# The head of a hybrid trunk kernel: squares summed on VectorE, one norm chain, GpSimd's elementwise work moved, and a step-size chain moved one weight pair later

## The chip, the cores and the metric

The kernel runs on one core of one Trainium2 chip. The metric is the device time of one execution in microseconds (us); a kernel is given by the median of its runs. Engines are named as in the profile: PE (TensorE matmuls), PEld (its weight loads), DVE (VectorE), ACT (ScalarE), POOL (GpSimd), SP (SyncE, which here only issues DMAs).

## The reference

One layer of a hybrid sequence model, on x of 1024 frames by 1024 channels, in float32, and a final RMSNorm. Cut to the part that the change touches:

```python
c_act = silu(c)
mod = (c_act @ w_ada + b_ada).reshape(1, 6, 1024)   # shift1, scale1, gate1, shift2, scale2, gate2
u = rms_norm(x, ln1) * (1.0 + scale1) + shift1
proj = u @ w_in                                      # 11296 columns: gates, conv, z, xBC, dt
...
dt = softplus(dt + dt_bias)
a = -exp(a_log)                                      # the state-space scan uses xs * dt and dt * a
```

Behind it come two mixers, two branch projections, the merge by gates, an output projection and an MLP of width 4096.

## The kernel before

Everything is held transposed: 128 channels on the partitions, 1024 frames along the free dimension, in two halves h of 512. x is eight channel tiles k of two halves each, 16 tiles `xt[k][h]`. A float32 matmul of full precision is made of three float32r matmuls: each operand is split into a high and a low part (`uh`, `ul` for u; `whi`, `wlo` for the weights), and high times high, high times low and low times high are added in PSUM (`mm3`, L108). The high part is a cast on ACT, the low part a subtraction on DVE.

The head, in the order of the code:

- L255 to L266: constants, and silu(c) broadcast to all partitions in `cb`.
- L276 to L279: SP issues the 16 loads of x and the two loads of the first modulation tile pair (`load_ada(0)`; each is 128 by 1024, 512 KB).
- L293 to L304: the norm, by half. `Stats.add` (L212) squares each of the eight tiles on ACT; for half 0 DVE adds the eight squares up in one tile, for half 1 POOL adds six of them and PE takes the last two as they are. `cols` (L205) sums over the partitions with matmuls of one column, 4 for each tile that it is given. Then a chain of some 11 small DVE operations (`rsqrt_eps`, L184: a seed and three Newton steps) gives 1/rms, DVE spreads it on a diagonal (`sdg`), a matmul with ones broadcasts it to all partitions, and ACT copies it to `rb`. So there are two such chains, one for each half. Behind that of half 0 stand three dummy matmuls (`WARM`).
- L312 to L332: the loop over the eight channel tiles j. Its modulation pair is loaded (four buffers, two for each j). `gemv` (L283) multiplies a 128 by 1024 tile of w_ada by `cb` and sums along the row, which gives shift or scale of 128 channels: for scale it is one DVE instruction, for shift from j = 1 on it is a POOL multiplication, an ACT pass that sums, and a small DVE operation. Then, for each half, DVE forms x times scale times `rb`, ACT adds the shift and casts it to `uh`, and DVE makes `ul`. In the first two rounds the weights of the first four feature tiles are split, with the low part on POOL. PE multiplies tile j of u by the four feature tiles (24 matmuls of 512 columns a round, 192 in all), into eight PSUM banks.
- L345 to L360: feature tiles 4 and 5 with `proj` (96 matmuls), while DVE and ACT make the operands of Strassen's scheme out of x (`tops_of` at L127, four DVE operations and four splits for each of four k; tiles named x and t).
- L362 to L383: the 32 dt columns: weights `wdr`, split to `wd`, 32 matmuls into `st`, then eight small matmuls (L383, 16 records) that turn the result and add its two parts.
- L392 to L412: softplus on a 128 by 256 tile as one DVE chain of about 25 operations, with two ACT passes near its start. It reads the PSUM tile `st` itself.
- L426 to L447: thirteen `strassen_pair`s (L135), for gates f = 6 to 15 and z. Each is seven products of 12 matmuls, with DVE sums of weight blocks (`s12`, `s34`), four weight splits and the evacuations. Between them stand three gemvs for each pair (`gemvs(3)`), out of 32 for the other four modulation vectors; they are loaded by POOL's DMA queue into one buffer `wv`.

Each engine takes its instructions strictly in the order of a list that is made when the kernel is built, by a planner that simulates the engines and takes, among the ready instructions of an engine, the one that stands first in the code. `tc.issue_after(i)` only adds an order: the instructions of the block on i's engine come behind i in its list.

Of the kernel before, what the change touches and what calls it, by code (L numbers as in the profile page):

```python
# [13 lines left out]
P = 128  # L14
T = 1024
# [7 lines left out]
WARM = 3  # L23
# [13 lines left out]
def hybrid_trunk(tc, xT, par, hrows, crow, wada1, wada2, win, wdt, wco, wso, wo, wup, wdn, out):  # L37
# [64 lines left out]
    def shift_split(hi, lo, src, col):  # L102
        act.activation(hi, src, AF.Identity, bias=col)
        stt(lo, src, col, hi.bitcast(F32), ALU.add, ALU.subtract)
# [166 lines left out]
    def load_ada(j):  # L271
        for q in (1, 0):
            wa[j, q] = p0.tile([P, T], F32, name="wada", bufs=4)
            sp.dma_start(wa[j, q], wada1[j, :, q])
# [4 lines left out]
    load_ada(0)  # L279
# [3 lines left out]
    def gemv(w_, o, eng):  # L283
        if eng is dve:
            dve.tensor_tensor_reduce(out=w_, in0=w_, in1=cb, scale=0.5, scalar=prm[:, BADA + o:BADA + o + 1],  # L285
                                     op0=ALU.mult, op1=ALU.add, accum_out=mcol[:, o:o + 1])
        else:
            tt(w_, w_, cb, ALU.mult, eng=pool)
            ga = p0.tile([P, 1], F32, name="ga")
            act.activation(w_, w_, AF.Copy, accum_out=ga)  # L290
            stt(mcol[:, o:o + 1], ga, 0.5, prm[:, BADA + o:BADA + o + 1], ALU.mult, ALU.add)

    rbs, sts = [], []  # L293
    for h in (0, 1):
        st = Stats(p0, ps0, pool if h else dve, 6 if h else 8, h)
        for k in range(KT):
            st.add(xt[k][h])
        rb = p0x.tile([P, H], F32, name=f"rb{h}")
        act.copy(rb, st.rb)
        rbs.append(rb)  # L300
        sts.append(st)
        if h == 0:
            for _ in range(WARM):
                pe.matmul(wps, lhsT=ones, rhs=xt[0][0], start=True, stop=True)  # L304
# [7 lines left out]
    for j in range(KT):  # L312
        if j:
            load_ada(j)
        if j in (0, 1):
            for f in range(2):
                ws.append(load_w(win[2 * j + f], eng=pool))
        with tc.issue_after((sts[0].dg if j else sts[0].last_add).ins):
            gemv(wa[j, 1], 8 + j, dve)
        gemv(wa[j, 0], j, pool if j else dve)  # L320
        stt(s1c[:, j:j + 1], mcol[:, 8 + j:9 + j], 1.0, prm[:, LN1 + j:LN1 + j + 1], ALU.add, ALU.mult)
        for h in (0, 1):
            x_ = xt[j][h]
            stt(x_, x_, s1c[:, j:j + 1], sts[0].rb if h == j == 0 else rbs[h], ALU.mult, ALU.mult)
            shift_split(uh[j][h], ul[j][h], x_, mcol[:, j:j + 1])
# [23 lines left out]
    for k in range(4):  # L349
        tks.append(tc.alloc_tile_pool(name=f"tk{k}", bufs=1, side="right", reuse_waits="tile"))  # L350
        for i, t in zip((0, 1, 2, 3), tops_of(xt[k] + xt[k + 4], mcol[:, 4 + k:5 + k], dc1[:, k:k + 1])):
# [42 lines left out]
    ev = sm("ev")
    act.activation(ev, v, AF.Abs)
    act.activation(ev, ev, AF.Exp, scale=-1.0)
    den = sm("den")
    tsc(den, ev, 2.0, None, ALU.add, ALU.bypass)
    dve.reciprocal(den, den)
    tt(ev, ev, den, ALU.mult)  # L400
    tt(z2, ev, ev, ALU.mult)
    tsc(den, z2, 2.0 / 19.0, 2.0 / 17.0, ALU.mult, ALU.add)
    for n in (15, 13, 11, 9, 7, 5, 3, 1):
        tt(den, den, z2, ALU.mult)
        tsc(den, den, 2.0 / n, None, ALU.add, ALU.bypass)
    tt(den, den, ev, ALU.mult)
    dtf = dt_t.rearrange("p c h -> p (c h)")
    stt(dtf, v, 0.0, den, ALU.max, ALU.add)
# [549 lines left out]
```

## Time and profile before

| | us |
|---|---|
| median of 3 runs (lowest, highest) | 2187.24 (2185.82, 2188.59) |
| the profiled execution's own time | 2188.47 |
| its span in the profile | 2186.7 |
| PE busy in the span | 2123.2 |
| DVE busy | 1409.7 |
| ACT busy | 876.8 |
| POOL busy | 146.1 |

The span runs from the first to the last instruction; 1.8 us of the execution's own time lie around it. Times of a row of the timeline are counted from the span's start. A row's second number is how long the instruction took, and the brackets, where there are any, say how long its engine had been idle and which event ended that. Windows of the trace give, for each engine, busy us and the number of instructions, then the clock that TensorE was granted (1.00 is full), the DMA engines' busy share and GB/s.

### The profile page before, as it was taken

The page shows a single profiled execution, that of the slowest core. Times are in us where ns is not written, and L with a number is a line of the kernel's source. Part 1 is how long each engine was busy: PE and PEld are TensorE (multiplying, and loading weights), DVE is VectorE, ACT ScalarE, POOL GpSimd, SP SyncE. Part 2 cuts the span into 40 slices and gives each one's busy share as a digit, 9 for nine tenths or more (in the row PEclk, how much of TensorE's full clock was granted, in tenths as well). Part 3 has the DMA queues.
Part 4 walks back from the last instruction along what each step waited for, and adds up shares of the span by engine and source line. Part 5 has one row for each costly group of instructions (what it writes and reads, how often), then busy time and mean ns, then how long its engine had stood idle before and what let it go on. Part 6 is the DMA issues. An engine that isn't in the chain of part 4 may idle for free.

```text
span 2186.7 us, 26107 instructions
## 1 busy us (share of the span) xinstructions
PE 2123.2 (97%) x9930; PEld 1734.7 (79%) x9930; DVE 1409.7 (64%) x2137; ACT 876.8 (40%) x1449; POOL 146.1 (7%) x216
## 2 busy tenths in 40 slices
PE   5989999999999999999999999999999999999998
PEld 3768778888888887888877888888788888888887
DVE  8947777664787767676785648746655545544444
ACT  4523333323565546364663421334445453211112
POOL 5100000000000000000000000021000000000003
PEclk7989999999999999999999999999999999999999
DMA  6325554223132322232347586543333336332212
GB/s 243 119 77 200 192 176 149 83 77 128 51 100 84 103 98 82 95 114 78 102 124 285 195 287 202 187 140 106 125 107 115 112 110 230 111 101 87 87 39 78
DMA packets 115471, 283.27 MB, mean 130 GB/s; under 512 B 10465, under 2 KB 45665, under 8 KB 115346
## 3 DMA queue, kind: packets, MB, share of 16 engines
q1 hardware_dynamic: 86882, 187.02, 26.7%
q0 software_dynamic: 16192, 58.73, 8.0%
q10 hardware_dynamic: 12272, 35.85, 4.2%
q8 instruction: 78, 1.28, 0.2%
q14 instruction: 47, 0.39, 0.1%
HBM read 218.45 MB, written 63.11 MB: 129 GB/s over the span
## 4 chain that ended last, share of the span: by engine, by line
PE 81%; issue 11%; DVE 5%; DMA 1%; POOL 1%; ACT 1%; SPq 0%; POOLq 0%; DVEq 0%; ACTq 0%
PE mm L144 21%; PE mm L113 18%; PE mm L111 18%; PE mm L110 18%; PE B L577 2%; PE B L582 1%; DVE x L45 1%; PE C L599 1%; PE A L554 1%; DMA wv<-in_wada 1%; DVE wada L285 1%; POOL wv L423 1%; DVE ul L45 1%; PE st L209 0%; DMA x<-in_xT 0%
## 5 line engine op out<-in xcount | busy, mean ns | idle before, releaser
L111 PE MATMUL mm<-ul,whi 128*128 128x512 f32 x768 | 304.9, 397 | 6.8 <-DVE ul L45 6.8
L144 PE MATMUL mm<-t,whi 128*128 128x512 f32 x944 | 294.4, 394 | 15.9 <-ACT whi L149 11.5
L110 PE MATMUL mm<-uh,whi 128*128 128x512 f32 x768 | 303.3, 397 | 2.5 <-ACT whi L93 2.5
L93 ACT CAST whi<-wraw 128x1024 fp32r<-128x1024 f32 x126 | 132.3, 1051 | 426.0 <-PE mm L111 402.1
L113 PE MATMUL mm<-uh,wlo 128*128 128x512 f32 x768 | 246.2, 396 | 0.1
L42 DVE TENSOR_TENSOR wlo<-wraw,whi 128x1024 fp32r<-128x1024 f32 (+1 forms) x188 | 212.0, 1128 | 41.2 <-ACT whi L93 35.1
L144 PEld LDWEIGHTS mm<-t,whi 128*128 128x128 f32 x944 | 179.0, 190 | 56.2 <-ACT whi L149 12.7
L45 DVE SCALAR_TENSOR_TENSOR y<-mm,mcol,y 128x512 f32<-128x512 f32 (+1 forms) x136 | 92.5, 716 | 157.6 <-PE mm L113 157.5
L144 PE MATMUL mm<-t,wlo 128*128 128x512 f32 x472 | 183.8, 391 | 0.0
L111 PEld LDWEIGHTS mm<-ul,whi 128*128 128x128 f32 x768 | 145.1, 189 | 36.9 <-DVE ul L45 7.7
L110 PEld LDWEIGHTS mm<-uh,whi 128*128 128x128 f32 x768 | 144.7, 189 | 33.9 <-ACT whi L93 3.3
L113 PEld LDWEIGHTS mm<-uh,wlo 128*128 128x128 f32 x768 | 144.7, 189 | 30.4 <-DVE wlo L42 0.5
L111 PE MATMUL mm<-hid,whi 128*128 128x512 f32 (+1 forms) x416 | 154.9, 374 | 0.0
L110 PE MATMUL mm<-hid,whi 128*128 128x512 f32 (+1 forms) x416 | 153.9, 373 | 0.0
L111 PE MATMUL mm<-ys,whi 128*128 128x512 f32 x384 | 148.5, 394 | 0.0
L110 PE MATMUL mm<-ys,whi 128*128 128x512 f32 x384 | 147.5, 395 | 0.6 <-ACT ys L99 0.5
L45 DVE SCALAR_TENSOR_TENSOR cacc<-raw,hw,cacc 128x1024 f32<-128x1024 f32 x96 | 122.8, 1279 | 27.9 <-ACT cacc L529 26.0
L144 PE MATMUL mm<-s,whi 128*128 128x512 f32 x448 | 137.8, 389 | 0.7 <-ACT cu L167 0.7
L113 PE MATMUL mm<-hid,wlo 128*128 128x512 f32 (+1 forms) x416 | 130.0, 373 | 0.0
L571 ACT ACTIVATE seg<-acb,acum 128x128 f32<-128x128 f32 x256 | 81.9, 392 | 102.6 <-PE B L577 95.0
L113 PE MATMUL mm<-ys,wlo 128*128 128x512 f32 x384 | 121.2, 390 | 0.0
L42 DVE TENSOR_TENSOR wlo<-s,whi 128x1024 fp32r<-128x1024 f32 x66 | 80.5, 1221 | 56.5 <-ACT whi L149 56.5
(269 smaller groups left out, 4027.8 us busy)
## 6 DMA issues: line engine op xcount, KB each, us to landing
wraw<-in_win SPq DMA_DIRECT2D x88, 512.0 KB, 3.5
wv<-in_wada POOLq DMA_DIRECT2D x32, 512.0 KB, 3.8
acb<-ac_d SPq DMA_DIRECT2D x64, 256.0 KB, 4.8
wraw<-in_wup SPq DMA_DIRECT2D x32, 512.0 KB, 3.6
hr<-hid_d POOLq DMA_DIRECT2D x32, 512.0 KB, 4.5
wraw<-in_wdn SPq DMA_DIRECT2D x32, 512.0 KB, 3.6
hid_d<-hid POOLq DMA_DIRECT2D x28, 512.0 KB, 4.0
gt<-gl_d SPq DMA_DIRECT2D x24, 512.0 KB, 4.2
```

What stands on the lines that cost most here:

```text
L42: return eng.tensor_tensor(out=o, in0=a, in1=b, op=op)
L45: return dve.scalar_tensor_tensor(out=o, in0=a, scalar=s, in1=b, op0=op0, op1=op1)
L93: act.copy(hi, raw)
L110: pe.matmul(o, lhsT=wh, rhs=h_, start=start, stop=False)
L111: pe.matmul(o, lhsT=wh, rhs=l_, start=False, stop=False)
L113: last_mm[0] = pe.matmul(o, lhsT=wl, rhs=h_, start=False, stop=stop)
L144: last_mm[0] = pe.matmul(o, lhsT=l_[:, s_], rhs=r_, start=first and k == j == 0, stop=k == 3 and j == 2, skip_group_check=True)
L285: dve.tensor_tensor_reduce(out=w_, in0=w_, in1=cb, scale=0.5, scalar=prm[:, BADA + o:BADA + o + 1], op0=ALU.mult, op1=ALU.add, accum_out=m ...
L423: pool.dma_start(w_, wada2[i])
L554: pe.matmul(A[:, 0:P], lhsT=bf[:, cs], rhs=cf[:, cs], start=True, stop=True)
L571: act.activation(seg[:, r, :], acb[:, r, :], AF.Relu, bias=acum[:, c, hd:hd + 1], scale=-1.0)
L577: pe.matmul(Bk[o:o + 64, P * (r // 2):P * (r // 2) + P], lhsT=xd[:, r, :], rhs=seg[:, r, :], start=True, stop=True, skip_group_check=True)
```

## The change

- The squares of both halves are summed on DVE, all eight tiles of each, with four buffers for squares. The column sums of both halves go into one PSUM tile of 8 columns, and one `rsqrt_eps` chain serves both. The diagonal and its broadcast stay by half. The dummy matmuls become four on x ahead of the sums and two on the last sum.
- All gemvs are the one DVE instruction; the low parts of the first four weight tiles are DVE's too. POOL has no elementwise work left in the head.
- Modulation tiles have eight buffers. `load_ada(0)` is issued between the two halves of x, and the first four weight tiles are loaded around `load_ada(1)`, the fourth into a buffer of its own.
- Orders are added: the low parts of the weights of round j and the gemvs of round j > 0 come on DVE behind the last `ul` of the round before (the first behind the diagonal of half 1), the casts of the second two weight tiles behind ACT's copy of the second `rb`, and the Strassen operands behind the last `ul`.
- The softplus chain is cut off behind the dt matmuls: ACT copies the PSUM result to `z2`, and the chain itself (`dt_chain`) is issued in the place of the gemvs at f = 8, in the buffer `wv`. There are no gemvs at f = 6 and 8, so three pairs of the gates and all eight of z carry them (9 + 23).

```diff
@@ -20,7 +22,6 @@
 NC_ = 8
 EPS = 1e-6
 RSQRT_SEED = 0x5F3759DF
-WARM = 3
 NYE = 4
 PARTS = ((0, 512, (1, 4, 6)), (512, 256, (1, 3, 4, 6)), (768, 256, (2, 5)))
@@ -101,7 +102,7 @@
     def shift_split(hi, lo, src, col):
         act.activation(hi, src, AF.Identity, bias=col)
-        stt(lo, src, col, hi.bitcast(F32), ALU.add, ALU.subtract)
+        return stt(lo, src, col, hi.bitcast(F32), ALU.add, ALU.subtract)
     last_mm = [None]
@@ -270,38 +271,56 @@
     def load_ada(j):
         for q in (1, 0):
-            wa[j, q] = p0.tile([P, T], F32, name="wada", bufs=4)
+            wa[j, q] = p0.tile([P, T], F32, name="wada", bufs=8)
             sp.dma_start(wa[j, q], wada1[j, :, q])
     for h in (0, 1):
         for k in range(KT):
             sp.dma_start(xt[k][h], xT[k, :, hs[h]])
-    load_ada(0)
+        if h == 0:
+            load_ada(0)
+    raws = [load_raw(win[f]) for f in (0, 1)]
+    load_ada(1)
+    raws.append(load_raw(win[2]))
+    raws.append(p0.tile([P, T], F32, name='wx', bufs=1))
+    sp.dma_start(raws[3], win[3])
     wps = mm.tile([P, H], F32, name="mm")
-    def gemv(w_, o, eng):
-        if eng is dve:
-            dve.tensor_tensor_reduce(out=w_, in0=w_, in1=cb, scale=0.5, scalar=prm[:, BADA + o:BADA + o + 1],
-                                     op0=ALU.mult, op1=ALU.add, accum_out=mcol[:, o:o + 1])
-        else:
-            tt(w_, w_, cb, ALU.mult, eng=pool)
...
-            stt(mcol[:, o:o + 1], ga, 0.5, prm[:, BADA + o:BADA + o + 1], ALU.mult, ALU.add)
-    rbs, sts = [], []
+    def gemv(w_, o):
+        return dve.tensor_tensor_reduce(out=w_, in0=w_, in1=cb, scale=0.5, scalar=prm[:, BADA + o:BADA + o + 1],
+                                        op0=ALU.mult, op1=ALU.add, accum_out=mcol[:, o:o + 1])
+    def warm(n, x_):
+        for _ in range(n):
+            pe.matmul(wps, lhsT=ones, rhs=x_, start=True, stop=True)
+    warm(4, xt[0][0])
+    st = ps0.tile([P, H], F32, name="st")
     for h in (0, 1):
-        st = Stats(p0, ps0, pool if h else dve, 6 if h else 8, h)
+        acc = None
         for k in range(KT):
-            st.add(xt[k][h])
+            sq = p0.tile([P, H], F32, name="ssq" if k else "sacc", bufs=4 if k else 2)
+            act.activation(sq, xt[k][h], AF.Square)
+            if k:
+                tt(acc, acc, sq, ALU.add)
+            else:
+                acc = sq
+        for j in range(4):
+            pe.matmul(st[:, 4 * h + j:4 * h + j + 1], lhsT=acc[:, j * P:j * P + P], rhs=ones[:, 0:1],
+                      start=h == j == 0, stop=True, skip_group_check=True)
+    warm(2, acc)
+    r = rsqrt_eps(p0, st[:, 0:8], 1.0 / T, [P, 8], "nst")
+    rbs = []
+    for h in (0, 1):
+        dg = p0.tile([P, 4, P], F32, name="sdg", bufs=1)
+        rdy = tt(dg, ident.unsqueeze(1).broadcast_to([P, 4, P]),
+                 r[:, 4 * h:4 * h + 4].unsqueeze(2).broadcast_to([P, 4, P]), ALU.mult)
+        ps = ps0.tile([P, H], F32, name="st")
+        pe.matmul(ps, lhsT=ones, rhs=dg.rearrange("p j t -> p (j t)"), start=True, stop=True)
         rb = p0x.tile([P, H], F32, name=f"rb{h}")
-        act.copy(rb, st.rb)
+        rbc = act.copy(rb, ps)
         rbs.append(rb)
-        sts.append(st)
-        if h == 0:
-            for _ in range(WARM):
-                pe.matmul(wps, lhsT=ones, rhs=xt[0][0], start=True, stop=True)
     ws = []
     sps = [[None, None] for _ in range(4)]
@@ -310,19 +329,20 @@
             pl, nm = (mm, "mm") if f < 2 else (ps0, ("sx", "st")[h])
             sps[f][h] = pl.tile([P, H], F32, name=nm)
     for j in range(KT):
-        if j:
+        if j > 1:
             load_ada(j)
         if j in (0, 1):
-            for f in range(2):
-                ws.append(load_w(win[2 * j + f], eng=pool))
-        with tc.issue_after((sts[0].dg if j else sts[0].last_add).ins):
-            gemv(wa[j, 1], 8 + j, dve)
-        gemv(wa[j, 0], j, pool if j else dve)
+            with tc.issue_after(rdy.ins), (tc.issue_after(rbc.ins) if j else contextlib.nullcontext()):
+                for f in range(2):
+                    ws.append(load_w(win[2 * j + f], raws[2 * j + f]))
+        with tc.issue_after(rdy.ins) if j else contextlib.nullcontext():
+            gemv(wa[j, 1], 8 + j)
+            gemv(wa[j, 0], j)
         stt(s1c[:, j:j + 1], mcol[:, 8 + j:9 + j], 1.0, prm[:, LN1 + j:LN1 + j + 1], ALU.add, ALU.mult)
         for h in (0, 1):
             x_ = xt[j][h]
-            stt(x_, x_, s1c[:, j:j + 1], sts[0].rb if h == j == 0 else rbs[h], ALU.mult, ALU.mult)
-            shift_split(uh[j][h], ul[j][h], x_, mcol[:, j:j + 1])
+            stt(x_, x_, s1c[:, j:j + 1], rbs[h], ALU.mult, ALU.mult)
+            rdy = shift_split(uh[j][h], ul[j][h], x_, mcol[:, j:j + 1])
         if j == 0:
             continue
         for jj in ((0, 1) if j == 1 else (j,)):
@@ -348,7 +368,9 @@
     tt(dc1, mcol[:, 4:8], mcol[:, 0:4], ALU.subtract)
     for k in range(4):
         tks.append(tc.alloc_tile_pool(name=f"tk{k}", bufs=1, side="right", reuse_waits="tile"))
-        for i, t in zip((0, 1, 2, 3), tops_of(xt[k] + xt[k + 4], mcol[:, 4 + k:5 + k], dc1[:, k:k + 1])):
+        with tc.issue_after(rdy.ins):
+            ts4 = tops_of(xt[k] + xt[k + 4], mcol[:, 4 + k:5 + k], dc1[:, k:k + 1])
+        for i, t in enumerate(ts4):
             o = [tks[-1].tile([P, H], F32R, name=f"t{i}{j}") for j in (0, 1)]
             split(*o, t)
             X[f"T{i + 1}"].append(o)
@@ -360,10 +382,6 @@
         gl_evac(f, proj(ws[f - 4], uh, ul))
     p0d = tc.alloc_tile_pool(name="p0d", bufs=1, reuse_waits="tile")
-    dtb = p0d.tile([P, NH], F32, name="dtb")
-    sp.dma_start(dtb, hrows[0].partition_broadcast(P))
-    alg = p0d.tile([P, NH], F32, name="alg")
-    sp.dma_start(alg, hrows[1].partition_broadcast(P))
     wdr = p0d.tile([P, KT, NH], F32, name="wdr")
     sp.dma_start(wdr, wdt)
     wd = p0d.tile([P, KT, 2 * NH], F32R, name="wd")
@@ -383,33 +401,7 @@
         pe.matmul(ps[:, c * NH:c * NH + NH], lhsT=dtT[:, c * P:c * P + P], rhs=sel, start=True, stop=True)
     C2 = NC_ * NH
-    def sm(name):
-        return p0d.tile([P, C2], F32, name=name)
-    def as3(a):
-        return a.rearrange("p (c h) -> p c h", c=NC_)
-    v = sm("v")
-    tt(as3(v), as3(ps[:, :C2]), dtb.unsqueeze(1).broadcast_to([P, NC_, NH]), ALU.add)
...
-    tsc(hb, prm[:, SCB:SCB + 32], 0.5, None, ALU.mult, ALU.bypass)
+    act.copy(z2, ps[:, :C2])
     p0d.release()
     ps0.release()
@@ -421,7 +413,35 @@
         for _, i in zip(range(n), gem):
             w_ = pe1.tile([P, T + 32], F32, name="wv", bufs=1)[:, 0:T]
             pool.dma_start(w_, wada2[i])
-            gemv(w_, 16 + i, dve)
+            gemv(w_, 16 + i)
+    def as3(a):
+        return a.rearrange("p (c h) -> p c h", c=NC_)
+    def dt_chain():
+        dc_ = pe1.tile([P, T + 32], F32, name="wv", bufs=1)
+        v, ev, den = [dc_[:, C2 * i:C2 * i + C2] for i in range(3)]
+        dtb, alg = dc_[:, 3 * C2:3 * C2 + NH], dc_[:, 3 * C2 + NH:3 * C2 + 2 * NH]
+        sp.dma_start(dtb, hrows[0].partition_broadcast(P))
+        sp.dma_start(alg, hrows[1].partition_broadcast(P))
+        tt(as3(v), as3(z2), dtb.unsqueeze(1).broadcast_to([P, NC_, NH]), ALU.add)
+        act.activation(ev, v, AF.Abs)
+        act.activation(ev, ev, AF.Exp, scale=-1.0)
+        tsc(den, ev, 2.0, None, ALU.add, ALU.bypass)
+        dve.reciprocal(den, den)
+        tt(ev, ev, den, ALU.mult)
+        tt(z2, ev, ev, ALU.mult)
+        tsc(den, z2, 2.0 / 19.0, 2.0 / 17.0, ALU.mult, ALU.add)
+        for n in (15, 13, 11, 9, 7, 5, 3, 1):
+            tt(den, den, z2, ALU.mult)
+            tsc(den, den, 2.0 / n, None, ALU.add, ALU.bypass)
+        tt(den, den, ev, ALU.mult)
+        dtf = dt_t.rearrange("p c h -> p (c h)")
+        stt(dtf, v, 0.0, den, ALU.max, ALU.add)
+        act.activation(alg, alg, AF.Exp)
+        stt(as3(z2), dt_t, -1.0, alg.unsqueeze(1).broadcast_to([P, NC_, NH]), ALU.mult, ALU.mult)
+        tsc(hw, prm[:, SCW:SCW + 128], 0.5, None, ALU.mult, ALU.bypass)
+        tsc(hb, prm[:, SCB:SCB + 32], 0.5, None, ALU.mult, ALU.bypass)
     for f in range(6, 16, 2):
         ts_ = [glp.tile([P, T], F32, name="glt") for _ in (0, 1)]
@@ -429,7 +449,10 @@
         def gl_ev(i, h, src):
             act.activation(ts_[i][:, hs[h]], src, AF.Tanh, scale=0.5)
-        gemvs(3)
+        if f == 8:
+            dt_chain()
+        elif f > 8:
+            gemvs(3)
         strassen_pair(pe1, win[f], win[f + 1], X, gl_ev)
         for i in (0, 1):
             act.dma_start(gl_d[f + i], ts_[i])
@@ -497,7 +520,7 @@
         v = p0e.tile([P, C2], F32, name="v")
         act.activation(v, ps[:, :C2], AF.Exp)
         act.activation(edec.rearrange("p c h -> p (c h)"), ps[:, C2:2 * C2], AF.Exp)
-        tt(de_t.rearrange("p c h -> p (c h)"), dtf, v, ALU.mult)
+        tt(de_t.rearrange("p c h -> p (c h)"), dt_t.rearrange("p c h -> p (c h)"), v, ALU.mult)
         acT = p0e.tile([NH, T], F32, name="acT", tag="dact")
         for h in (0, 1):
             ps = ps1.tile([P, H], F32, name="st")
```

More of the change, by code (lines that the diff above doesn't have):

```diff
@@ L1 @@
+import contextlib
 import concourse.bass as bass
@@ L278, in hybrid_trunk @@
             sp.dma_start(xt[k][h], xT[k, :, hs[h]])
-    load_ada(0)
-    wps = mm.tile([P, H], F32, name="mm")
-    def gemv(w_, o, eng):
-        if eng is dve:
-            dve.tensor_tensor_reduce(out=w_, in0=w_, in1=cb, scale=0.5, scalar=prm[:, BADA + o:BADA + o + 1],
-                                     op0=ALU.mult, op1=ALU.add, accum_out=mcol[:, o:o + 1])
-        else:
-            tt(w_, w_, cb, ALU.mult, eng=pool)
-            ga = p0.tile([P, 1], F32, name="ga")
-            act.activation(w_, w_, AF.Copy, accum_out=ga)
-            stt(mcol[:, o:o + 1], ga, 0.5, prm[:, BADA + o:BADA + o + 1], ALU.mult, ALU.add)
@@ L384, in hybrid_trunk @@
     C2 = NC_ * NH
-    def sm(name):
-        return p0d.tile([P, C2], F32, name=name)
-    def as3(a):
-        return a.rearrange("p (c h) -> p c h", c=NC_)
-    v = sm("v")
-    tt(as3(v), as3(ps[:, :C2]), dtb.unsqueeze(1).broadcast_to([P, NC_, NH]), ALU.add)
[L394 to L408, printed above, removed]
-    act.activation(alg, alg, AF.Exp)
-    stt(as3(z2), dt_t, -1.0, alg.unsqueeze(1).broadcast_to([P, NC_, NH]), ALU.mult, ALU.mult)
-    tsc(hw, prm[:, SCW:SCW + 128], 0.5, None, ALU.mult, ALU.bypass)
-    tsc(hb, prm[:, SCB:SCB + 32], 0.5, None, ALU.mult, ALU.bypass)
+    act.copy(z2, ps[:, :C2])
     p0d.release()
```

## The prediction

> **What bounds the kernel now.** First the page and the windows, to see whether PE is the bound everywhere.
>
> ```profile
> PE 2123.2 (97%) x9930; PEld 1734.7 (79%) x9930; DVE 1409.7 (64%) x2137; ACT 876.8 (40%) x1449; POOL 146.1 (7%) x216
> ```
> ```profile
> 20.00:40.00 20.00, 10.31 (x34) 8.16 (x34) 18.55 (x25) 5.79 (x8) 13.48 (x5) 0.59 0.69 241
> 40.00:60.00 20.00, 12.36 (x35) 8.31 (x36) 19.58 (x25) 8.71 (x14) 8.42 (x3) 0.71 0.44 141
> 140.00:160.00 20.00, 12.20 (x48) 9.97 (x49) 18.57 (x33) 4.51 (x5) 1.79 (x3) 0.82 0.37 115
> 349.00:420.00 71.00, 71.00 (x315) 58.82 (x314) 48.14 (x67) 25.02 (x33) 0.00 (x0) 1.00 0.31 111
> ```
>
> From 349 to 420 PE is busy all the time, 71.00/315 = 0.225 us a matmul at full clock. In the head it is not: half idle, at a low clock, while DVE is full (19.58 of 20). So the head is DVE's. Which waits, the list of PE's waits over the whole span says:
>
> ```profile
> PE st L232 <- DVE sdg L42: 19.9, 3, 9.3
> PE mm L144 <- ACT whi L149: 11.5, 2, 8.0
> PE mm L111 <- DVE ul L45: 6.8, 2, 6.7
> PE mm L144 <- DVE cq L42: 4.4, 4, 3.0
> ```
>
> Three of the four lie ahead of 148 us: the norm's diagonal, the wait for u, and 8.0 us ahead of the first Strassen products. Only the last belongs to the pairs. And DVE's full state is not all work; the timeline and the groups between 20 and 106 us show its instructions stretched:
>
> ```profile
> 21.27 1.28 DVE L285 CUSTOM_DVE_ANT_0 wada<-wada,cb,prm 128x1024 f32<-128x1024 f32 x1
> 25.12 5.13 POOL L42 TENSOR_TENSOR wlo<-wraw,whi 128x1024 fp32r<-128x1024 f32 x2 [5.18 <-ACT whi L93]
> 27.96 3.38 DVE L285 CUSTOM_DVE_ANT_0 wada<-wada,cb,prm 128x1024 f32<-128x1024 f32 x1
> 42.67 0.75 DVE L45 SCALAR_TENSOR_TENSOR x<-x,s1c,rb 128x512 f32<-128x512 f32 x1 [0.35 <-DVE s1c L45]
> ```
> ```profile
> L45 DVE SCALAR_TENSOR_TENSOR x<-x,s1c,rb 128x512 f32<-128x512 f32 x15 | 19.1, 1309 | 0.4 <-DVE s1c L45 0.4
> L285 DVE CUSTOM_DVE_ANT_0 wada<-wada,cb,prm 128x1024 f32<-128x1024 f32 x9 | 15.7, 1744 | 0.0
> L45 DVE SCALAR_TENSOR_TENSOR ul<-x,mcol,uh 128x512 fp32r<-128x512 f32 x16 | 13.1, 841 | 0.8 <-ACT uh L103 0.8
> ```
>
> The same gemv takes 1.28 us with POOL idle and 3.38 beside a POOL subtraction; the scaling of x takes 0.75 alone and 1.309 in the mean. The Trainium skill (SBUF — State Buffer, Who interferes with whom) says that a DVE instruction with two SBUF inputs and a GpSimd one that reads SBUF exclude each other, and the later one blocks fully; these rows agree.
>
> **The change part by part.** I rebuild the head's time line with undisturbed durations, as POOL computes nothing there any more.
>
> ```profile
> 0.00:17.50 17.50, 10.05 (x18) 4.18 (x18) 9.24 (x19) 10.00 (x17) 5.08 (x12) 0.90 0.86 304
> ```
> ```profile
> 6.12 5.12 PE L304 MATMUL mm<-x,ones 128*128 128x512 f32 x6
> 12.70 0.69 DVE L42 TENSOR_TENSOR sacc<-sacc,ssq 128x512 f32<-128x512 f32 x1 [0.53 <-ACT ssq L216]
> 14.74 0.16 DVE L48 TENSOR_SCALAR nst<-st 128x4 f32<-128x4 f32 x1 [1.35 <-PE st L209]
> 20.66 0.69 DVE L42 TENSOR_TENSOR sdg<-ident,nst 128x512 f32<-128x512 f32 x1
> 39.05 0.16 DVE L42 TENSOR_TENSOR nst<-nst 128x4 f32<-128x4 f32 x1
> 39.64 0.16 DVE L42 TENSOR_TENSOR nst<-nst 128x4 f32<-128x4 f32 x1
> 21.40 2.08 PE L232 MATMUL st<-sdg,ones 128*128 128x512 f32 x2 [6.70 <-DVE sdg L42]
> 23.52 0.59 ACT L299 COPY rb<-st 128x512 f32<-128x512 f32 x1 [2.91 <-PE st L232]
> 24.94 0.72 ACT L103 ACTIVATE uh<-x,mcol 128x512 fp32r<-128x512 f32 x1
> 28.25 0.77 PE L110 MATMUL mm<-uh,whi 128*128 128x512 f32 x1
> 40.98 2.08 PE L232 MATMUL st<-sdg,ones 128*128 128x512 f32 x2 [9.26 <-DVE sdg L42]
> ```
>
> *Start of u.* One chain for both halves must wait for all of x, and `load_ada(0)` now stands ahead of half 1: 4.2 MB of x, 1.05 of modulation and 0.15 of parameters, 5.4 MB. At 304 GB/s that is 17.8 us; I take 18.5, since later loads share the engines. A last square (about 0.6, as ACT's copy of that shape) and a last addition of 0.69: 19.8. Column sums 1.35: 21.2. The chain: three Newton steps of 0.59 (39.05 to 39.64) and two operations of 0.2, 2.2 us, where the first chain of before took 5.9 (14.74 to 20.66, beside POOL): 23.4. Diagonal 0.69, broadcast 2.08, copy 0.59: 26.8. The two new dummy matmuls (1.7 each by the six records of 5.12) hold PE until 24.6 at the worst, 0.5 late; the four early ones lie under the loads. Meanwhile DVE makes the second diagonal and two `wlo`, about 3 us of cover. Gemv j = 0 fits under the loads if its place in DVE's list allows, else 2.6 more. Then x of half 0, 0.75, `uh` 0.72: PE's first matmul on u at about 28.4, and round 0 leaves DVE at 29.6. Before, it was 28.25, but PE then idled 9.26 us up to 40.98, for the second diagonal.
>
> *The rounds.*
>
> ```profile
> 86.51 2.06 DVE L45 SCALAR_TENSOR_TENSOR x<-x,dc,x 128x512 f32<-128x512 f32 x3
> 102.62 2.49 DVE L42 TENSOR_TENSOR t<-x,t 128x512 fp32r<-128x512 f32 x4
> L42 DVE TENSOR_TENSOR wlo<-wraw,whi 128x1024 fp32r<-128x1024 f32 x3 | 3.6, 1217 | 0.0
> 94.50 0.39 PE L113 MATMUL st<-uh,wlo 128*128 128x512 f32 x1
> 119.96 0.40 PE L376 MATMUL st<-uh,wd 128*64 128x512 f32 x1
> ```
>
> A run of three shows 0.69 each for the three-operand form, a run of four 0.62 for the subtraction. A round is two gemvs of 1.28 and four such of 0.69, 5.3; with the small ones I take 5.4. PE's share of a round is 24 × 0.225 = 5.4 too, so they run in step. Two more `wlo` of 1.22 follow round 0 (32.0), then seven rounds: 69.8. Seven gemvs, four `wlo` and seven additions are new on DVE (9.0 + 4.9 + 4.8 = 18.7 us) and are in this sum. The Strassen operands, tied behind, leave it. PE ends its 192 matmuls one round after the last round's first `uh`, about 74.5; from below, 28.4 + 43.2 and 1.5 for a first stretch at half clock is 73.1. Before, that end was 94.9: a gain of 20.4. All loads of this stretch are 14.8 MB, 49 us at 304 GB/s, where the last pair is wanted at 64: no wait, with 15 us of cover.
>
> *Tiles 4 and 5 and dt.* From 94.9 to 119.96 PE took 25.1, gaps at the weight casts included; kept, it reaches dt at 99.6. Now DVE may be late there: 12 × 0.69 + 20 × 0.62 + 3 × 1.22 = 24.3 us behind 69.8, then `wdr`, whose load was issued only as the operands ended:
>
> ```profile
> 104.19 0.67 SPq L368 DMA_DIRECT2D wdr<-in_wdt  x1
> 109.33 0.43 DVE L42 TENSOR_TENSOR wd<-wdr,wd 128x256 fp32r<-128x256 f32 x1 [4.13 <-ACT wd L370]
> 127.33 0.39 PE L144 MATMUL mm<-uh,whi 128*128 128x512 f32 x1
> 132.51 0.42 DVE L42 TENSOR_TENSOR v<-st,dtb 128x256 f32<-128x256 f32 x1 [22.75 <-PE st L383]
> 144.44 0.42 DVE L45 SCALAR_TENSOR_TENSOR z<-dt_t,alg 128x256 f32<-128x256 f32 x1
> 147.81 2.50 PE L144 MATMUL mm<-t,whi 128*128 128x512 f32 x5 [7.95 <-ACT whi L149]
> ```
>
> That path is 104.19 to 109.76, 5.6: 99.7. The two meet, cover 0. The dt matmuls take 7.4 (to 127.33): 107.1; the first product and the turning 5.2 (to 132.51): 112.3.
>
> *The softplus chain.* Before, DVE worked on it from 132.51 to 144.86, and the first `s12`, cast and product came 2.95 behind it. Now the 2.95 follow 112.3 directly, with PE's second product (12 × 0.225 = 2.7) under them: PE resumes at 115.3, where before it did at 147.81. Gain 32.5. The copy to `z2` is one ACT instruction like L299, hidden.
>
> *What comes back.* The 12.4 us of chain go to pair f = 8:
>
> ```profile
> 166.70:185.60 18.90, 18.90 (x85) 15.63 (x85) 13.61 (x20) 6.15 (x10) 1.59 (x3) 1.00 0.63 201
> ```
>
> A pair is 18.9 us for PE, with 13.6 of DVE, of which three gemvs are 3.9. Without those in pairs 6 and 8, DVE has 9.2 free in each, 18.4 for a chain of 12.4, so it is mostly covered; but the code of pair 8 stands behind it in DVE's list, and its first `wlo` and `s12` can be late. Bounds 0 and 12.4; I take 3, as the free time nearly covers it. The gemvs move to the last two z pairs, where before the wait for cq came in some pairs with gemvs: 4.4 over eleven, 0.4 a pair; two pairs of the wider z evacuation, 1.5 (0 to 3). SP's queue gets the two small loads of the chain later, POOL's queue nothing at f = 6 and 8.
>
> Sum: 2188.5 − 32.5 + 3 + 1.5 = 2160.5, against the profiled execution's 2188.47, which is 1.2 above the median of its runs; I say 2160.
>
> **The rivals.** *a. The chain stands whole in front of pair 8.* Its price is 12.4 in place of 3: 2169.9. For it: DVE's list is strict, and the chain stands first in the code. Against: the free 9.2 in pair 6.
>
> *b. DVE is saturated and gets nothing back.* If the long rows came not from POOL, a round costs 2 × 1.744 + 2 × 1.309 + 2 × 0.841 = 7.8, 2.4 more in each of eight, 19.1: 2179.6. The Trainium skill (Perfetto Trace Analysis, Optimizing Scalar/DVE Operations) speaks for such a reading: with DVE saturated, moving work to ScalarE or even GpSimd may make sense, and this change does the opposite; the same section warns that the two share a port. The 1.28 beside 3.38 speaks against the rival.
>
> *c. Slower: the pairs' evacuation queues behind all that is hung on DVE ahead of it.* Ten pairs with three gemvs (38.4), one with two (2.6) and the chain (12.4) make 53.4, less the 4.4 already paid: 2188.5 − 32.5 + 49 = 2205.0. It is slower from the point where 69% of the 53.4 is uncovered (36.9). Against: before, 41 us of gemvs cost 4.4.
>
> *d. Better.* Gemv 0 and the chain wholly covered, DVE at 5.3 a round, no new z wait: 2188.5 − 34.5 = 2154 or a little less.
>
> **How the numbers follow.** Forecast 0.66 (own range 2155 to 2167: chain 0 to 8, start late by up to 2.6); a 0.15; d 0.08; b 0.05; c 0.04; 0.02 for smaller slips that leave no change. About 0.2% (4.4 us) is what a measurement can tell here. Faster 0.93, same 0.03, slower 0.04. The range takes in a and d: 2150 to 2173.
>
> **What would show it.** Right: no DVE gemv above 1.4 us in the head; PE's first matmul on u near 28, unbroken from about 37; f0 to f3 ended near 74; dt near 100; no 8 us gap ahead of the first t product; that product near 115. Wrong: a gap at dt (operands late), a gap of over 5 us at the start of pair 8 (a), cq waits above 1 us in most pairs (c), long gemvs without POOL (b), or a first matmul on u behind 33.

## The result, and the profile after

The changed kernel takes 2163.95 us (median of 4 runs, 2160.25 to 2165.64), the kernel before 2187.91 (4 runs, 2185.82 to 2190.66): ratio 0.9887, 95% interval 0.987 to 0.9905. It is faster, 4 us above the predicted 2160.0 and inside the range. The profiled execution took 2164.64 us, with a span of 2162.9. In helpers the changed kernel's line numbers are one higher than before.

First the engines' line of the page after, then PE's waits over its whole span (in all, times, longest):

```profile
PE 2121.5 (98%) x9920; PEld 1731.0 (80%) x9920; DVE 1398.5 (65%) x2144; ACT 869.2 (40%) x1436; POOL 108.9 (5%) x200
```
```profile
PE st L310 <- DVE sacc L43: 8.1, 2, 5.6
PE mm L145 <- ACT whi L150: 4.4, 1, 4.4
PE st L233 <- DVE sdg L43: 4.0, 1, 4.0
PE mm L111 <- ACT uh L104: 3.2, 1, 3.2
PE mm L145 <- DVE cq L43: 3.0, 5, 1.3
...
PE mm L114 <- DVE wlo L43: 1.9, 1, 1.9
PE mm L145 <- ACT cu L168: 1.6, 2, 0.9
```

Of the 19.9 us of waiting for a diagonal 16.0 are gone, and with them the 6.8 for `ul` and the 8.0 ahead of the first Strassen products. (The waits of 4.0 for `sdg` and 4.4 for `whi` in this list lie behind 400 us, where the kernel before has 4.0 and 3.6.) Up to the first product on `t` PE now waits for the sums, for `uh`, 1.9 us for the low part of a weight tile and 0.9 for `cu`. The windows of after (span, busy time and count of PE, PEld, DVE, ACT and POOL, granted clock, DMA share, GB/s):

```profile
20.00:40.00 20.00, 15.05 (x38) 9.49 (x39) 14.72 (x30) 6.52 (x9) 0.00 (x0) 0.65 0.93 354
40.00:60.00 20.00, 20.00 (x89) 16.06 (x88) 19.37 (x33) 5.42 (x8) 0.00 (x0) 1.00 0.43 146
78.90:106.80 27.90, 25.51 (x102) 19.73 (x101) 19.92 (x31) 14.51 (x27) 0.00 (x0) 0.94 0.38 138
140.00:160.00 20.00, 20.00 (x90) 16.57 (x89) 18.15 (x35) 7.26 (x10) 1.26 (x2) 1.00 0.47 158
```

POOL is at 0.00 in the head. From 40 to 60 us PE is full at full clock (20.00 and 1.00 for 12.36 and 0.71 before), and DVE is as full as it was (19.37), but its rows are short. The groups of after between 30 and 90 us (busy us, mean ns of one):

```profile
L291 DVE CUSTOM_DVE_ANT_0 wada<-wada,cb,prm 128x1024 f32<-128x1024 f32 x14 | 17.4, 1280 | 0.0
L46 DVE SCALAR_TENSOR_TENSOR x<-x,s1c,rb 128x512 f32<-128x512 f32 x16 | 11.3, 748 | 0.2
```

The gemv means 1280 ns (1744 before), the scaling of x 748 (1309). The largest loss against the forecast lies at the start of u. DVE's timeline of after there, and further rows of it that the point-by-point reading uses:

```profile
14.26 1.28 DVE L291 CUSTOM_DVE_ANT_0 wada<-wada,cb,prm 128x1024 f32<-128x1024 f32 x1
15.46 5.46 DVE L43 TENSOR_TENSOR sacc<-sacc,ssq 128x512 f32<-128x512 f32 x7
...
22.88 0.17 DVE L49 TENSOR_SCALAR nst<-st 128x8 f32<-128x8 f32 x1 [1.96 <-PE st L310]
...
25.16 0.69 DVE L43 TENSOR_TENSOR sdg<-ident,nst 128x512 f32<-128x512 f32 x1
27.84 0.69 DVE L43 TENSOR_TENSOR sdg<-ident,nst 128x512 f32<-128x512 f32 x1 [1.99 <-PE st L320]
28.45 2.35 DVE L43 TENSOR_TENSOR wlo<-wraw,whi 128x1024 fp32r<-128x1024 f32 x2
30.72 1.41 DVE L46 SCALAR_TENSOR_TENSOR x<-x,s1c,rb 128x512 f32<-128x512 f32 x2
...
83.01 1.22 DVE L43 TENSOR_TENSOR wlo<-wraw,whi 128x1024 fp32r<-128x1024 f32 x1
...
98.98 0.42 DVE L43 TENSOR_TENSOR wd<-wdr,wd 128x256 fp32r<-128x256 f32 x1 [0.59 <-ACT wd L388]
...
120.36 0.42 DVE L43 TENSOR_TENSOR wv<-z,wv 128x256 f32<-128x256 f32 x1
...
151.66 0.42 DVE L46 SCALAR_TENSOR_TENSOR z<-dt_t,wv 128x256 f32<-128x256 f32 x1
```

The second diagonal stands 1.99 us, because its one buffer is still to be read by the first broadcast. Behind it in DVE's list stand two `wlo`, and only then the scaling of x, at 30.72. ACT's timeline of after shows that the broadcast row was ready at 28.43, and that two weight casts stand ahead of `uh`:

```profile
14.74 4.68 ACT L304 ACTIVATE ssq<-x 128x512 f32<-128x512 f32 x7
...
27.84 0.59 ACT L322 COPY rb<-st 128x512 f32<-128x512 f32 x1 [5.50 <-PE st L320]
...
30.23 1.05 ACT L94 CAST whi<-wraw 128x1024 fp32r<-128x1024 f32 x1
31.18 1.05 ACT L94 CAST whi<-wx 128x1024 fp32r<-128x1024 f32 x1
32.12 1.33 ACT L104 ACTIVATE uh<-x,mcol 128x512 fp32r<-128x512 f32 x2
```

And PE's timeline of after:

```profile
22.70 3.76 PE L296 MATMUL mm<-sacc,ones 128*128 128x512 f32 x4
26.25 1.55 PE L320 MATMUL st<-sdg,ones 128*128 128x512 f32 x2
...
32.90 1.22 PE L111 MATMUL mm<-uh,whi 128*128 128x512 f32 x2 [3.19 <-ACT uh L104]
...
84.28 0.73 PE L114 MATMUL mm<-uh,wlo 128*128 128x512 f32 x2 [1.87 <-DVE wlo L43]
...
105.95 0.39 PE L145 MATMUL mm<-uh,whi 128*128 128x512 f32 x1
...
106.86 0.40 PE L394 MATMUL st<-uh,wd 128*64 128x512 f32 x1
...
123.85 1.55 PE L145 MATMUL mm<-t,whi 128*128 128x512 f32 x6
```

The two dummy matmuls on the last sum (four records) held PE until 26.25, and the broadcast waited behind them; its diagonal was ready at 25.85, so that cost 0.4 us. The first product on `t` comes at 123.85, where before it came at 147.81: 23.96 earlier. The medians differ by 23.96 too, so behind this point nothing is won or lost on balance.

### The profile page after: what moved, and what is told of

The parts are those of the page before. It is cut to its first block, busy times and chain, and to the rows that moved or that the text cites. A ratio compares the mean times of both kernels' runs of the same rounds, so it can differ in the third digit from the quotient of the medians.

```text
span 2162.9 us, 26045 instructions
## 1 busy us (share of the span) xinstructions
PE 2121.5 (98%) x9920; PEld 1731.0 (80%) x9920; DVE 1398.5 (65%) x2144; ACT 869.2 (40%) x1436; POOL 108.9 (5%) x200
## 4 chain that ended last, share of the span: by engine, by line
PE 81%; issue 11%; DVE 3%; DMA 2%; ACT 1%; POOL 1%; SPq 0%; POOLq 0%; DVEq 0%; ACTq 0%
PE mm L145 21%; PE mm L112 18%; PE mm L111 18%; PE mm L114 18%; PE B L600 2%; PE B L605 1%; PE C L622 1%; DMA wv<-in_wada 1%; DVE wada L291 1%; PE A L577 1%; DMA x<-in_xT 1%; POOL wv L415 1%; DVE ul L46 1%; DVE x L46 0%; DMA hr<-hid_d 0%
```

## The experiments

Each is timed against the kernel before in the same session (its medians: 2186.93 to 2187.57). Most kernels start from the changed one.

**The two halves of the change.** *chain_only* is the kernel before, with only the softplus chain (and its two loads) moved to f = 8 and the three gemvs at f = 6 and 8 dropped to later pairs. *head_only* is the changed kernel with the chain back in its old place and gemvs in every pair:

```diff
-        gemvs(3)
+        if f == 8:
+            dt_chain()
+        elif f > 8:
+            gemvs(3)
```

> The kernel before with the softplus chain alone moved to pair 8; the head and POOL's work stay. Theory (two gains that add up): the 15.3 us between the last turning matmul and the first t product (132.5 to 147.8) shrink to about 3, so 11 to 13 us less than before, about 2176, and no new wait in pair 8. Rival 1 (the head's gain is all, the chain is hidden in any place): within 3 us of before. Rival 2 (the chain's bill comes due in pair 8): 3 us less than before or none, with a PE wait of 8 us or more at the start of pair 8.

> The changed kernel with the softplus chain back in its old place and gemvs in every pair from f = 6; only the head is changed. Theory: the 24.0 us less chain_only's part, so 11 to 13 us less than before, about 2176, with dt beginning near 107 as in the changed kernel. Rival (the head gives nearly all): 20 us or more less than before. Rival (the head gives little): under 5 us.

chain_only: 2177.44 us, ratio 0.9954 (0.9941 to 0.9968). head_only: 2177.18, ratio 0.9952 (0.9939 to 0.9964). PE's timeline of chain_only, and that of head_only:

```profile
136.33 1.52 PE L144 MATMUL mm<-t,whi 128*128 128x512 f32 x6
```
```profile
133.46 2.93 PE L145 MATMUL mm<-t,whi 128*128 128x512 f32 x6 [7.96 <-ACT whi L150]
```

By the medians each half is worth some 10 us, a little less than the 11 to 13 that were expected. At the first product on `t` the chain's move is worth 11.5 us and the head 14.4, where both together gave 23.96. The 8 us wait belongs to the chain: it stays in head_only. In spans, 11.0 and 11.3 of 23.8 were left. Each half meets a later wait that is some 2.5 us longer than before; the list of PE's waits in chain_only shows it:

```profile
PE A L555 <- DVE xe L42: 3.8, 1, 3.8
```

Before it was 1.4, in head_only it is 4.0, in the changed kernel it is absent. It lies in work that none of the edits touch, behind 400 us. The planner orders that work anew for each kernel. What makes or removes this wait was not found out: each kernel has one trace, and executions of one kernel differ by up to 7.6 us (2171.98 to 2179.55 for head_only), so it may belong to the order or to the one execution. A few us of any total here are of this kind.

**Is it POOL's work that stretches DVE's?** *pool_reads* gives POOL one multiplication a round that reads two tiles in SBUF and whose result nobody uses; *pool_writes* gives it three memsets a round in its place.

```diff
+        tt(scr, wa[j, 1], cb, ALU.mult, eng=pool)      # pool_reads
+        for _ in range(3):                             # pool_writes
+            pool.memset(wa[j, 1], 0.0)
```

> The changed kernel, and in each of the eight rounds one POOL multiplication of 128 by 1024 with two SBUF inputs (the used modulation tile and cb) into a scratch tile that nobody reads; DVE's order in the rounds is the same. Theory (POOL instructions that read SBUF stop DVE's two-input instructions): each takes about 2.5 to 3.3 us and stretches the round by some 1.7, so 10 to 18 us slower than the changed kernel, near 2178, gemvs or x rows above 2 us. Rival (the stretched rows of before were waits for data or buffers, and POOL only stood beside them): within 2 us of the changed kernel, gemvs at 1.28.

> The changed kernel, and in each of the eight rounds three POOL memsets of 128 by 1024 on the used modulation tile: POOL is busy as long, but reads nothing from SBUF. Theory: within 2 us of the changed kernel, DVE rows unstretched. Rival (any POOL instruction that touches SBUF stops DVE, or POOL's semaphores do): as pool_reads, 10 us or more slower.

pool_reads: 2178.79, ratio 0.9961 (0.9947 to 0.9974), 14.8 us over the changed kernel. pool_writes: 2160.85, ratio 0.9878 (0.9865 to 0.9892), no slower. Groups of pool_reads between 20 and 90 us:

```profile
L43 POOL TENSOR_TENSOR scr<-wada,cb 128x1024 f32<-128x1024 f32 x7 | 23.1, 3295 | 49.3 <-DVE mcol L291 49.3
L46 DVE SCALAR_TENSOR_TENSOR s1c<-mcol,prm 128x1 f32<-128x1 f32 x7 | 16.3, 2333 | 0.0
L46 DVE SCALAR_TENSOR_TENSOR x<-x,s1c,rb 128x512 f32<-128x512 f32 x16 | 11.3, 748 | 0.2
```

and the same of pool_writes, where POOL is nearly as busy:

```profile
L342 POOL MEMSET wada<- 128x1024 f32 x21 | 20.1, 955 | 37.6 <-DVE mcol L291 36.8
...
L291 DVE CUSTOM_DVE_ANT_0 wada<-wada,cb,prm 128x1024 f32<-128x1024 f32 x14 | 17.4, 1278 | 0.0
...
L46 DVE SCALAR_TENSOR_TENSOR s1c<-mcol,prm 128x1 f32<-128x1 f32 x7 | 1.1, 153 | 0.0
```

The whole stretch falls on the smallest instruction: `s1c`, one column, takes 2333 ns in place of 153, 15.2 us over seven rounds, about as much as the kernel lost (the multiplication of the eighth round stands ahead of this window). One round in pool_reads' timeline shows how:

```profile
39.55 1.28 DVE L291 CUSTOM_DVE_ANT_0 wada<-wada,cb,prm 128x1024 f32<-128x1024 f32 x1
39.78 3.28 POOL L43 TENSOR_TENSOR scr<-wada,cb 128x1024 f32<-128x1024 f32 x1 [23.12 <-DVE mcol L291]
...
40.76 2.32 DVE L46 SCALAR_TENSOR_TENSOR s1c<-mcol,prm 128x1 f32<-128x1 f32 x1
```

The gemv that already runs isn't slowed; the next DVE instruction with two inputs in SBUF is held until POOL's ends (43.06 and 43.08). The expectation had named the gemvs and the scaling of x as the victims; those rows stayed at their undisturbed length, so that part missed. The Trainium skill (SBUF — State Buffer, Who interferes with whom) says that a DVE instruction with two SBUF inputs contends with a GpSimd instruction that reads SBUF and not with one that only writes. Both runs agree. So rival b, that the long rows were DVE's own, falls. The Trainium skill (Perfetto Trace Analysis, Optimizing Scalar/DVE Operations) allows that handing work of a full DVE to GpSimd may make sense, and warns that between these two it might not help. These runs bear out the warning: eight POOL multiplications, seven of them 23.1 us by their rows, cost 14.8 us of the total.

**What else in the head is a term?** *no_ties* takes out the three `issue_after`; *four_bufs* gives the modulation tiles four buffers for eight; *two_chains* builds one norm chain for each half again, both summed on DVE.

```diff
-            with tc.issue_after(rdy.ins), (tc.issue_after(rbc.ins) if j else contextlib.nullcontext()):
+            with contextlib.nullcontext():           # no_ties, and so at the other two ties
-            wa[j, q] = p0.tile([P, T], F32, name="wada", bufs=8)
+            wa[j, q] = p0.tile([P, T], F32, name="wada", bufs=4)     # four_bufs
-    r = rsqrt_eps(p0, st[:, 0:8], 1.0 / T, [P, 8], "nst")
+        r = rsqrt_eps(p0, st[:, 0:4], 1.0 / T, [P, 4], "nst")   # two_chains, in the loop over h
```

> The changed kernel without its ties: the weight splits of the first two rounds, the gemvs and the Strassen operands may stand anywhere in DVE's list. DVE's list then has eight gemvs and four weight splits between the last square and the first ul, four of them inside the norm's chain. Theory (the start of u decides as PE and DVE keep step behind it): PE's first matmul on u near 39 in place of 32.9, some of it won back as later rounds have fewer gemvs; 3 to 5 us slower than the changed kernel, 2167 to 2169. Rival (the order does not matter, DVE's sum of work does): within 1 us. Rival (ties only hold work back): faster.

> The changed kernel with four modulation buffers in place of eight; DVE's order is the same. Theory: a pair is loaded again when its gemvs are done, two rounds (11 us) ahead of its use, and lands in 4 to 6.5 us; no change, within 2 us of the changed kernel, no DVE wait on a modulation load over 1 us. Rival (the eight buffers are what took the loads off DVE's path): 5 us or more slower with DVE waiting for loads in each round.

> The changed kernel with a norm chain for each half, as before, but all on DVE; the second chain adds 2.2 us to DVE. Theory (half 1 of round 0 waits for all of x either way, and DVE's instructions stand in one order): first matmul on u some us earlier, the second rb at 29 to 31 as in the changed kernel; within 1.5 us of the changed kernel. Rival (one chain for both halves is a main term of the gain): 3 us or more slower. Rival (waiting for all of x costs what the prediction's start lost): 3 us or more faster.

A word on places first. The start of dt is not quite the same point in all kernels: the planner put 4 of the 12 matmuls of the first Strassen product ahead of it in the changed kernel (the row at 105.95 is one), all 12 in operand_ties and late_operands below, none in no_ties, early_split and less_dve. At full clock 4 take 0.9 us and 12 take 2.7. The first product on `t` is the safer mark.

no_ties: 2162.06, ratio 0.9889 (0.9872 to 0.9906): the same as the changed kernel, though PE's first matmul on u comes only at 39.14, 6.2 later. The start came where it was expected, but the slower kernel that was expected with it did not: the time comes back at tiles 4 and 5, as this window of no_ties shows:

```profile
84.80:107.00 22.20, 22.20 (x99) 18.09 (x98) 6.79 (x10) 7.79 (x15) 0.00 (x0) 1.00 0.48 173
```

There PE runs unbroken and reaches dt at 106.98 (106.86 in the changed kernel) and the first product on `t` at 123.30 (123.85). DVE is busy for only 6.79 of these 22.20 us, as it did the operands and the low parts earlier. The ties move about 6 us of PE's waiting from one place to the other. four_bufs: 2162.83, ratio 0.9887 (0.9872 to 0.9902): eight buffers are no term. two_chains: 2169.14, ratio 0.9916 (0.9902 to 0.9929), 5.2 us over the changed kernel by the medians (the intervals just touch), where no change was expected. Its DVE timeline, and two rows of PE's:

```profile
21.89 0.69 DVE L43 TENSOR_TENSOR sdg<-ident,nst 128x512 f32<-128x512 f32 x1
26.93 0.75 DVE L46 SCALAR_TENSOR_TENSOR x<-x,s1c,rb 128x512 f32<-128x512 f32 x1 [4.35 <-ACT rb L322]
```
```profile
21.38 3.78 PE L296 MATMUL mm<-sacc,ones 128*128 128x512 f32 x4 [5.83 <-DVE sacc L43]
24.95 1.33 PE L320 MATMUL st<-sdg,ones 128*128 128x512 f32 x2
```

Here u starts earlier (28.49), but DVE is empty for 4.35 us while the dummy matmuls and the first broadcast run, and the second half's chain comes behind that; PE leaves the rounds some 2.7 us later (81.99 for 79.25) and reaches the first product on `t` 3.55 later (127.40). The rest of the 5.2 comes behind that point, where the `xe` wait is 4.0 and the changed kernel has none. And 2.4 of the 4.35 us are the dummy matmuls', which in this kernel stand ahead of the first broadcast while its diagonal is ready at 22.58. So two chains in this form are slower, but what the second chain costs without the dummies ahead of the broadcast was not measured: that one chain serves both halves is a likely term of the gain, of unknown size.

**The start of u.** *two_diagonals* gives `sdg` a second buffer. *early_split* has that, puts the first weight's low part right behind the last addition, and the casts of weights 2 and 3 behind the first `uh`.

```diff
-        dg = p0.tile([P, 4, P], F32, name="sdg", bufs=1)
+        dg = p0.tile([P, 4, P], F32, name="sdg", bufs=2)
...
+            for f in range(2):                             # early_split
+                with tc.issue_after((rdy if j or f else last_add).ins), (tc.issue_after(last_uh[0].ins) if j else contextlib.nullcontext()):
+                    ws.append(load_w(win[2 * j + f], raws[2 * j + f]))
```

> The changed kernel with two buffers for the diagonal. In the changed kernel the second diagonal waits 2.0 us for PE to read the first, with the weight splits and the scaling of x behind it. Theory: x of round 0 about 2 us earlier (28.8 in place of 30.7), all of it kept to the end: 2 us less than the changed kernel, near 2162. Rival (the first matmul is bound by ACT's casts of the second two weight tiles or by the weights' loads): less than 0.5 us.

> The changed kernel with two diagonals, the first weight split tied behind the last square's addition in place of the second diagonal, and the casts of the second two weight tiles behind the first uh in place of the second rb. Theory: PE's first matmul on u at 29.5 to 30 in place of 32.9, so 3 us less than the changed kernel, near 2161, and below two_diagonals by 1. Rival (the split in front of the chain delays the diagonal by as much): same as two_diagonals.

two_diagonals: 2160.36, ratio 0.988 (0.9864 to 0.9895). early_split: 2160.06, ratio 0.9875 (0.986 to 0.989). The first matmul on u moves from 32.90 to 32.02 and to 30.82, dt from 106.86 to 104.42 and 104.09, the first product on `t` from 123.85 to 121.18 and 120.40. In the first, ACT's two casts ahead of `uh` take the place of the diagonal's wait. In the second those casts and the first low part are out of the way and DVE waits 1.13 us for `rb`; the start still comes about 1 us later than was expected. Both intervals overlap that of the changed kernel, so the totals alone show no gain; the places do.

**DVE's sum of work, and its order.** *less_dve* leaves out the shift gemvs of rounds 1 to 7 (the shift of those channels stays zero): 9.0 us less of DVE work in the rounds, with one memset ahead of them. *operand_ties* puts the Strassen operands of k = 1 behind the low part of tile 4 in DVE's list, and those of k = 2 and 3 behind that of tile 5 (`lo4` and `lo5` in the cut). *late_operands* has these ties and all of early_split.

```diff
-            gemv(wa[j, 0], j)                # less_dve
+            if j == 0:
+                gemv(wa[j, 0], j)
...
-        with tc.issue_after(rdy.ins):        # operand_ties
+        with tc.issue_after((rdy, lo4, lo5, lo5)[k].ins):
             ts4 = tops_of(xt[k] + xt[k + 4], mcol[:, 4 + k:5 + k], dc1[:, k:k + 1])
```

> The changed kernel without the shift gemvs of rounds 1 to 7: shift is left at zero for these channels, seven DVE instructions of 1.28 us (9.0 us) are gone, the loads stay. Theory (DVE and PE are both full in the rounds, 5.48 and 5.4 us, so a lighter DVE leaves PE as the bound): the rounds end at 77 to 78 in place of 79.2, the operands 7 to 9 us earlier, tiles 4 and 5 lose their wait; 4 to 7 us less than the changed kernel, near 2158. Rival (DVE alone bounds the head up to dt): 9 us less. Rival (PE alone bounds it): 2 us less or none.

> early_split, and the Strassen operands of k = 1 tied on DVE behind the low part of weight tile 4, those of k = 2 and 3 behind that of tile 5. In the changed kernel PE waited 1.9 us for the first of these low parts at 82.4, behind operands, and then ran 3.9 us at half clock. Theory (the 5.4 us that tiles 4 and 5 take beyond 21.6 are that wait and its clock): dt starts at 100 to 101 in place of 104.1 in early_split, 3 to 4 us less than early_split, near 2157. Rival (DVE's sum of work bounds the end of the head: what is not waited for at tile 4 is waited for at the dt weights): dt at 103 or later, within 1 us of early_split.

> The changed kernel with the operand ties of late_operands alone: the operands of k = 1 stand behind the low weight part of tile 4 in DVE's list, those of k = 2 and 3 behind that of tile 5; the single diagonal buffer and the order of the first weight splits stay as the change has them. Theory (the wait for the low part of tile 4 and the slow stretch behind it are a loss of their own, about 3 us up to dt): the first matmul on u stays near 32.9, the rounds end on PE near 79, the wait for wlo is gone, dt starts near 104 (106.86 in the changed kernel), the first t product near 119 to 120, and the whole is 3 to 6 us faster than the changed kernel, about 2158 to 2161. Rival 1 (most of the 7.8 us between late_operands and early_split came from the order of later parts that the planner chose anew, not from the ties): dt and the first t product as above, but the total within 2 us of the changed kernel's. Rival 2 (DVE's sum of work is the limit, so the operands are only late later): no wlo wait, but a wait of about 2 us at dt or at the first t product, and the first t product within 1.5 us of 123.85.

less_dve: 2153.31, ratio 0.9841 (0.9828 to 0.9855), 10.6 us under the changed kernel. The first matmul on u and the rounds' end on PE stay where they were (33.41 and 79.48 for 32.90 and 79.25), though the rounds were expected to end at 77 to 78: with the rows short, PE sets the pace of the rounds, and DVE is full beside it. The wait for `wlo` is gone, dt starts at 101.08 for 106.86 and the first product on `t` comes at 117.43, 6.4 earlier. So what PE lost at tiles 4 and 5 hung on how much stands in DVE's list ahead of their low parts. 9.0 us off that list are worth 6.4 there; the other 4 us of the total come behind this point and are not explained.

operand_ties: 2157.72, ratio 0.9869 (0.9853 to 0.9886). late_operands: 2152.28 (5 runs, 2149.43 to 2153.09), ratio 0.9837 (0.9823 to 0.985), which is faster than both kernels. The window of operand_ties over the stretch shown for the changed kernel, and one of late_operands:

```profile
78.90:106.80 27.90, 27.85 (x123) 22.02 (x122) 20.29 (x32) 15.32 (x27) 0.00 (x0) 1.00 0.44 157
```
```profile
78.00:90.00 12.00, 12.00 (x54) 9.94 (x53) 12.00 (x19) 9.95 (x18) 0.00 (x0) 1.00 0.70 261
```

PE is full at full clock, with DVE as busy (20.29 for 19.92): the same work in another order. operand_ties reaches dt at 103.95, and by then it has done 8 more matmuls of the first product (1.8 us) than the changed kernel, so tiles 4 and 5 are 4.7 us shorter, where about 3 were expected. The first product on `t` comes at 117.22, 6.6 us before the changed kernel. It then meets the later wait again:

```profile
PE A L581 <- DVE xe L43: 4.4, 1, 4.4
```

The theory of a loss of its own at tiles 4 and 5 holds, and both rivals fall at that place; its total alone would not settle it, as the intervals overlap. late_operands has the first product at 115.72, 8.1 us earlier than the changed kernel, and a span that is 12.2 shorter. Of the other 4.1, 1.8 is a wait for `gt` behind 400 us that the changed kernel has and late_operands has not, and 1.0 a shorter wait for `whi` there, while the waits for `cq` are 1.2 longer. That these come from the planner's new order and not from the edit is likely, not shown; the rest of the 4.1 is open.

## Why the prediction was right, and where it was off

The total came out 4.1 us above the sum for the profiled execution (2164.64 for 2160.5). That is a loss of 8.55 up to the first product on `t` (123.85 for 115.3) less 4.5 that were to come back and did not. One reading of the list of waits was loose: it put the 19.9 us for the diagonal ahead of 148 us, where 4.0 of them lie behind 400; the sum does not use it.

- *Start of u, 28.4 forecast, 32.90 measured: +4.5, the largest miss.* 1.6 of it lie ahead of the first `rb`, which is there at 28.43 for 26.8. The last addition ends at 20.92, not 19.8: seven additions follow each other every 0.8 us from 15.46, where ACT makes a square every 0.67. Gemv 0 did fit under the loads, as the prediction hoped: its second instruction ends at 15.54, and the square that the first of these additions needs at 15.37. The column sums took 1.96 for 1.35, the chain 2.28 for 2.2, and the dummy matmuls the 0.4 that the prediction allowed ("0.5 late"); the broadcast was 0.5 shorter. What failed is the step behind the broadcast. The prediction had the second diagonal and two `wlo` as "about 3 us of cover". The runs showed that this cover stands *ahead* of the scaling of x in DVE's list and is itself held by the single diagonal buffer, which costs 2.3 us from `rb` to the scaling, and that ACT's casts of weights 2 and 3 stand ahead of `uh`, 0.65 more. two_diagonals and early_split took 0.9 and 2.1 of the 4.5 away.
- *The rounds: 5.4 forecast.* From the first matmul to the rounds' end on PE are 46.35 us, where 46.1 were forecast. PE and DVE are both full, PE unbroken up to the end. Right; less_dve adds that PE is the one that sets the pace.
- *Tiles 4 and 5: 25.2 forecast (74.5 to 99.7), 27.6 measured (79.25 to 106.86), +2.4.* 0.9 of the 27.6 are the four matmuls of the first product ahead of dt. The prediction kept the stretch of before and asked only whether operands and dt weights would be late at its end. They were not (`wd` at 98.98). What was late is the low part of tile 4, in the middle, behind operands that nobody needed yet: PE waits 1.87, and its clock is at 0.94 in the mean. operand_ties removes both, and 4.7 us with them, more than the miss: the stretch of before that was kept had waits of its own (22.51 us busy of 25.07).
- *dt to the first product: 15.6 forecast, 17.0 measured, +1.4.* The softplus chain is off the path, as chain_only shows alone (16.3). In the 17.0 are a wait of 0.95 for `cu`, which chain_only has too, and a stretch at half clock from 119.4 to 122.5: the last 12 matmuls ahead of the first product on `t` take 4.45 us from 119.40, and 2.89 in operand_ties, where the clock is full.
- *What comes back: 4.5 forecast, about 0 measured, on balance.* The chain's instructions, from 120.36 to 151.66, are spread among the weight sums, low parts and evacuations of the pairs, and from 120 to 200 us PE is busy throughout (80.00 of 80). The waits for `cq` are 3.0 in five, below the 4.4 of before. The bound from below was the better value: DVE's list is strict, but the planner mixes the chain into the free slots and does not put it whole in front of the pair. Rivals a and c fall. That the balance is so near 0 is partly luck: the `xe` wait of 1.4 to 4.4 us that several kernels have is absent here, and a `gt` wait of 1.8 is new.

So the main mechanisms were right: DVE's rows were long because of POOL's reads, they are short now and the rounds are full, and the softplus chain is off PE's path. Wrong were the cover at the start of u, whose 32.90 lies just short of the 33 that was named as a sign of being wrong, and the wait in the middle of tiles 4 and 5, which had no term. These losses and the chain's cheaper cover have opposite signs, and that the total came out closer than its terms is luck in part. No run tried the order of the loads, the number of dummy matmuls or the move of POOL's work alone in the kernel before; how the head's part divides among them is open.

## What to carry to other kernels

Where an engine is full in the trace, ask first whether its rows have their undisturbed length: here some 14 us of DVE's full state (15 × 0.56 of the scaling of x, 9 × 0.46 of the gemvs, 16 × 0.09 of `ul`) was in rows longer than the same rows with POOL idle, and pool_reads shows that POOL's reads can do that. A change that took work from POOL *onto* the full engine made the kernel faster. Cover is only cover when it stands behind the critical instruction in its engine's list; look for what is queued ahead of it (a diagonal in a single buffer, casts for weights that are wanted later, operands that are wanted 20 us later). When the order of the work is planned anew with each edit, compare kernels at a point just behind the edit as well as at the end, because later waits of 2 to 4 us come and go.

## What was not expected of the hardware

Beside a POOL multiplication of 3.3 us a one-column DVE instruction took 2.33 us in place of 0.153; in the mean, 23.1 us of POOL rows that read cost 15.2 us of DVE, while 20.1 us of POOL's memsets cost none. PE's clock fell after a short stop: behind the wait of 1.87 us at 84.28 the window from 85.0 to 89.3 us has a granted clock of 0.60 with PE busy throughout; from 82 to 85 us PE had been busy for 1.13 of 3.00. After a wait of 0.95 us it fell once (0.51 from 119.4 to 122.5, in the changed kernel) and not in operand_ties, which has the same wait; what decides between these is open.
